# Modulation products in groups of four over the column quarters of TensorE, with a third weight buffer in the gating stage

## The chip, the cores and the metric

The kernel runs on one core of one Trainium2 chip, in one launch. The metric is the device time of that launch in microseconds (us). The time before is the median of three runs, 3602.42 us (3598.81 to 3608.07).

The engines are TensorE (PE; its weight loads are PEld), VectorE (DVE), ScalarE (ACT), GpSimd (POOL) and SyncE (SP). SP and POOL issue the DMAs that this text is about.

## What is computed

Two blocks of layers over 512 tokens of width 1024, all in float32. The first block is an attention layer (`mla`), a feed-forward layer, a spatial gating layer (`sgu`) and a second feed-forward layer. The second block has four layers (convolution, a linear recurrence, attention, convolution) over the 512 tokens and 256 context tokens. Each of these four takes a shift, a scale and a gate from a conditioning vector, and that modulation is what the change touches:

```python
def second_block(x, c, ctx, c_ctx, norm_g, mod_w, mod_b, ...):
    for i in range(DEPTH_2):                       # 4 layers
        shift, scale, gate = modulation(c, mod_w[i], mod_b[i])
        h = modulate(rmsnorm(x, norm_g[i]), shift[:, None], scale[:, None])
        if ctx_in:
            shift_c, scale_c, gate_c = modulation(c_ctx, mod_w[i], mod_b[i])
        ...
        x = x + gate[:, None] * y
```

`modulation` multiplies silu(c), 1024 numbers, with a matrix 1024 x 3072 and adds a bias; `c_ctx` goes the same way. For the four layers that is 4 x 12.6 MB of weights for very little arithmetic.

## The kernel before

Features lie on the 128 partitions, in 8 tiles (KT = 8). Most products are made in three float32r parts: the helper `wblk` (lines 87 to 97) loads a block of weights 128 x 1024 (0.5 MB) by SP, splits it on ACT (L93) and DVE (L94), and `mm3` (L121 to L123) multiplies high with high, high with low and low with high. One block is 24 matmuls of 128 x 512 (in `mla` some are fewer, in `sgu` one loop is written out, L754).

The modulation is a side stream. It does not depend on the tokens, so `set_filler` (lines 278 to 287) makes it a generator that each `wblk` of the main chain advances: by two steps in `mla` (layer 0 of the second block), by one step in `sgu` and the second feed-forward layer (layers 1 to 3, one after the other). Its weights are issued by POOL (L84, the helper `load`) into the pool `wst` of the side stream: three buffers in `mla`, two in `sgu`.

```python
    def modulation(self, s, l, pool, ps):                       # L302
        for k in range(KT):
            for b in range(3):
                w = s.load(A["mod_w"][l, k, :, b * 1024:(b + 1) * 1024])
                for h in range(2):
                    n = 2 * b + h
                    q = n % 4
                    nc.tensor.matmul(pm[n // 4][32 * q:32 * q + 32, :], self.cs[:, k, :], w[:, h * 512:(h + 1) * 512],
                                     start=k == 0, stop=k == KT - 1, skip_group_check=True)     # L312
                yield 1
```

A load holds 1024 of the 3072 columns for 128 input features. Each half of it is one product (L312): the stationary operand is `cs`, 128 x 32 (two of its 32 columns are the two vectors, the rest zero), the moving one 128 x 512 of the weights. The 32 output rows go to one of four groups of 32 partitions, q = 0 to 3, and with that the product uses one quarter of the array's columns. The six products of one k are q = 0 and 1, q = 2 and 3 in the PSUM tile `pm[0]`, and q = 0 and 1 in `pm[1]`. A float32 product stands in the trace as two matmul records, so two products are "x4" there. There are 4 layers x 24 loads x 2 = 192 products, 96 pairs.

At the end of a layer, ACT copies `pm` to SBUF (L318), four transposes for each of the two tiles follow (L321), and DVE adds the bias (L323).

The program is not in the order in which the code emits it: a scheduler inside the framework places each instruction on its engine's queue by its own estimates. Each engine then works through its queue in that fixed order, so a product that is not ready holds up what stands behind it on PE.

Other lines that the text names: L171 (`colsum`) and L180 (`rows`) are the two TensorE ends of a norm, with a chain of small DVE steps between them (L205, L156 to L162); L436 is a memset by POOL for the convolution that follows.

Of the kernel before, what the change touches and what calls it, by code (L numbers as in the profile page):

```python
# [7 lines left out]
F32 = mybir.dt.float32  # L8
F32R = mybir.dt.float32r
I32 = mybir.dt.int32  # L10
AF = mybir.ActivationFunctionType
# [6 lines left out]
KT = 8  # L18
# [33 lines left out]
class Stream:  # L52
    """Pools and helpers for a chain of layers over N tokens, features on the partitions."""
# [8 lines left out]
    def pools(self, nm, wst=0, whl=0, hp=0, tp=0, mm=0, W=None, hw=None):  # L62
        """Opens the pools that are asked for by their buffers."""
# [23 lines left out]
    def wblk(self, src, cols=1024, st=None):  # L87
        """A block of weights in float32, split exactly into two float32r parts."""
# [14 lines left out]
    def split(self, pr, src, scale=None, bias=None):  # L103
        """hi + lo = src * scale, or src + bias"""
# [20 lines left out]
    def lin(self, outs, w, acts, wo=0, ws=P, start=True, stop=True):  # L125
        """outs: [(PSUM part, columns of the tokens)]"""
        n = len(acts)
        for k, a in enumerate(acts):
            ww = tuple(x[:, wo + k * ws:wo + k * ws + P] for x in w)
            for o, c in outs:  # L130
                self.mm3(o, ww, (a[0][:, c], a[1][:, c]), start and k == 0, stop and k == n - 1)
# [9 lines left out]
    def group(self, ws, acts):  # L141
        """Several outputs at once, as the operands become ready."""
# [6 lines left out]
    def rsqrt(self, v, pool=None):  # L149
        """v ** -0.5 on a small tile [128, n]"""  # L150
# [14 lines left out]
    def colsum(self, tiles, N):  # L165
        """Sums over the features for each token: PSUM [128 tokens, N / 128]."""
# [8 lines left out]
    def rows(self, y, N, tag="rs", dst=None):  # L175
        """Columns y [128 tokens, N / 128] -> a row over all partitions [128, N]; in PSUM without a tag."""
# [33 lines left out]
class Kern:  # L210
# [17 lines left out]
    def open_x(self, n):  # L228
        """The two streams and the running sums of their squares."""
# [12 lines left out]
    def track(self, k, vi=0, acc=None, gain=1.0):  # L242
        """x[:, k] is final: its squares go into the sum for the next norm."""
# [14 lines left out]
    def both_rstd(self, s):  # L258
        """The norms of x and of the context in one chain."""
# [18 lines left out]
    def set_filler(self, gen, per=1):  # L278
        """Another chain of work, emitted in step with the blocks of weights of the main one."""
# [14 lines left out]
    # ------------------------------------------------------------- modulation  # L294
# [7 lines left out]
    def modulation(self, s, l, pool, ps):  # L302
        """shift, scale and gate of layer l, for both vectors, with the features on the partitions"""
        nc, A = self.nc, self.A
        pm = [ps.tile([P, 512], F32, name=f"pmod{i}", bufs=1) for i in range(2)]
        for k in range(KT):
            for b in range(3):
                w = s.load(A["mod_w"][l, k, :, b * 1024:(b + 1) * 1024])
                for h in range(2):
                    n = 2 * b + h  # L310
                    q = n % 4
                    nc.tensor.matmul(pm[n // 4][32 * q:32 * q + 32, :], self.cs[:, k, :], w[:, h * 512:(h + 1) * 512],  # L312
                                     start=k == 0, stop=k == KT - 1, skip_group_check=True)
                yield 1
        for g in range(2):
            nq = 4 if g == 0 else 2
            r = pool.tile([P, 512], F32, name="modr")
            nc.scalar.activation(out=r[:32 * nq], in_=pm[g][:32 * nq], func=AF.Copy)  # L318
            pt = ps.tile([P, 4, P], F32, name=f"pmod{g}", bufs=1)
            for j in range(4):  # L320
                nc.tensor.transpose(pt[:, j, :32 * nq], r[:32 * nq, j * P:(j + 1) * P], self.ident[:32 * nq, :32 * nq])  # L321
            for vi in range(2):
                nc.vector.tensor_tensor(  # L323
                    out=self.modv[:, l, vi, 16 * g:16 * g + 4 * nq].rearrange("p (q j) -> p q j", j=4),
                    in0=pt[:, :, :32 * nq].rearrange("p j (q r) -> p q j r", r=32)[:, :, :, vi],
                    in1=self.v("mod_b", 24 * l + 16 * g, 4 * nq).rearrange("p (q j) -> p q j", j=4), op=ALU.add)
# [5 lines left out]
    def mod_h(self, s, x, l, vi, rs=None, gs=None):  # L332
        """The modulated norm of x, split."""
# [17 lines left out]
    # -------------------------------------------------------------- conv layer  # L351
    def conv(self, s, x, l, j, vi):
# [3 lines left out]
        with self.tc.tile_pool(name=f"cv{N}", bufs=1, side=s.side, reuse_waits="tile") as cp, \  # L356
# [5 lines left out]
            for k in range(KT):  # L362
# [10 lines left out]
                # twice a * sigmoid(b)  # L373
# [18 lines left out]
            # layer norm over the features  # L392
# [25 lines left out]
            # the norm that the next layer starts from takes the place of the sums  # L418
# [3 lines left out]
    def conv_x(self, l, j):  # L422
        """The layer on x. The convolution runs in PSUM: some taps as diagonal matrices on TensorE, most on VectorE; the last ones are for ScalarE and GpSimd."""
        nc, A, s, x, N, H = self.nc, self.A, self.m, self.x, T, 15
        NPE, NPO, NG = 4, 7, 4
        with self.tc.tile_pool(name="cv", bufs=1, reuse_waits="tile") as cp, self.tc.tile_pool(name="cw", bufs=5, reuse_waits="tile") as cw, \
# [7 lines left out]
            def glu(k):  # L434
# [7 lines left out]
                # twice a * sigmoid(b)  # L442
# [60 lines left out]
            # layer norm over the features  # L503
# [23 lines left out]
    # ---------------------------------------------------------------- block 1  # L527
    def scaled(self, gname, gi):
        """x * gain, split"""
# [15 lines left out]
    def mla(self):  # L545
        nc, tc, A, s = self.nc, self.tc, self.A, self.m
        scale = 192.0 ** -0.5
        with tc.tile_pool(name="mla", bufs=1, reuse_waits="tile") as mp, tc.tile_pool(name="mla2", bufs=2, reuse_waits="tile") as m2, \
# [10 lines left out]
            # the first products wait in PSUM for the norm  # L559
# [6 lines left out]
            # rope tables: cos and signed sin of fl(position * inv_freq)  # L566
# [160 lines left out]
    def sgu(self):  # L727
        nc, tc, A, s = self.nc, self.tc, self.A, self.m
        with tc.tile_pool(name="sgu", bufs=1, reuse_waits="tile") as sp, tc.tile_pool(name="sgu2", bufs=2, reuse_waits="tile") as s2, \
                tc.tile_pool(name="sgu8", bufs=9, reuse_waits="tile") as s8, s.pools("m", hp=8, tp=2, mm=2), tc.tile_pool(name="pa", bufs=1, space=PSUM, reuse_waits="tile") as pa:  # L730
            # spatial weights, masked, and the sums of their rows
# [76 lines left out]
    def final_norm(self, s):  # L808
        """The norm at the end of the first block, and in one step with it the norm of the layer that follows."""
# [6 lines left out]
        # r1 = (m1 + eps) ** -0.5 and r1 * (r1 ** 2 * m2 + eps) ** -0.5 = (m2 + eps * (m1 + eps)) ** -0.5  # L816
# [16 lines left out]
    # -------------------------------------------------------------- rwkv layer  # L833
    # tokens of both sequences side by side: 256 of the context, then 512 of x; two halves of 384 in two banks
# [1067 lines left out]
```

## Time and profile before

| | |
|---|---|
| median of three runs | 3602.42 us |
| lowest, highest | 3598.81, 3608.07 us |
| span of the profiled execution | 3582.6 us |
| what lies around the span, against the median | 19.8 us |
| PE busy | 3409.4 us, 95% |
| DVE, ACT, POOL busy | 64%, 40%, 17% |

The profiled execution has no time of its own beside its span; the 19.8 us is the difference to the median. The page gives each engine's busy time, the span in 40 slices, the DMA queues, and groups of instructions by line. Matmuls are pipelined: one of 512 columns shows some 0.39 us, while the next starts 0.23 us after it, so distances between starts are what a matmul costs, not its length. "idle before <-" names what ended the wait of the engine.

Where the stages lie, in us from the span's start: `mla` to about 250, with its modulation products from 8 to 112; the first feed-forward layer to about 690; `sgu` to 1045; the second feed-forward layer to 1424, with modulation products to 1211.

### The profile page before, as it was taken

The page shows a single profiled execution, that of the slowest core. Times are in us where ns is not written, and L with a number is a line of the kernel's source. Part 1 is how long each engine was busy: PE and PEld are TensorE (multiplying, and loading weights), DVE is VectorE, ACT ScalarE, POOL GpSimd, SP SyncE. Part 2 cuts the span into 40 slices and gives each one's busy share as a digit, 9 for nine tenths or more (in the row PEclk, how much of TensorE's full clock was granted, in tenths as well). Part 3 has the DMA queues.
Part 4 walks back from the last instruction along what each step waited for, and adds up shares of the span by engine and source line. Part 5 has one row for each costly group of instructions (what it writes and reads, how often), then busy time and mean ns, then how long its engine had stood idle before and what let it go on. Part 6 is the DMA issues. An engine that isn't in the chain of part 4 may idle for free. (4 is left out here: it accounts for less than half of the span.)

```text
span 3582.6 us, 52130 instructions
## 1 busy us (share of the span) xinstructions
PE 3409.4 (95%) x20784; PEld 2778.1 (78%) x20784; DVE 2307.9 (64%) x3811; ACT 1448.9 (40%) x2336; POOL 603.8 (17%) x674
## 2 busy tenths in 40 slices
PE   7999999999999999998999979999889999999897
PEld 4678888767766787676988858888788788888676
DVE  4568875426443345887478788888452476666786
ACT  3443334323232233555356524333423254444553
POOL 1000000000000000763002231121110200000682
PEclk9999999999999999998999879999899999999999
DMA  6123333343444322221227772221421522211221
GB/s 246 44 89 107 111 117 113 136 142 136 152 143 157 120 98 94 71 77 65 95 101 227 240 208 82 84 87 49 175 92 42 182 71 80 71 62 46 91 73 57
DMA packets 201380, 396.94 MB, mean 111 GB/s; under 512 B 16624, under 2 KB 109552, under 8 KB 200112
## 3 DMA queue, kind: packets, MB, share of 16 engines
q1 hardware_dynamic: 161328, 287.56, 24.0%
q0 software_dynamic: 24880, 93.08, 7.8%
q10 hardware_dynamic: 14928, 12.98, 1.2%
q8 instruction: 163, 2.67, 0.3%
q14 instruction: 81, 0.66, 0.1%
HBM read 328.79 MB, written 58.46 MB: 108 GB/s over the span
## 5 line engine op out<-in xcount | busy, mean ns | idle before, releaser
L93 ACT ACTIVATE wh<-wst 128x1024 fp32r<-128x1024 f32 (+1 forms) x413 | 423.0, 1026 | 1100.5 <-PE pmm L122 728.8
L121 PE MATMUL pmm<-hh,wh 128*128 128x512 f32 (+1 forms) x1752 | 670.5, 384 | 4.2 <-ACT hh L108 3.6
L123 PE MATMUL pmm<-hh,wl 128*128 128x512 f32 (+1 forms) x1752 | 662.3, 379 | 4.3 <-POOL wl L94 4.3
L122 PE MATMUL pmm<-hl,wh 128*128 128x512 f32 (+1 forms) x1752 | 661.5, 378 | 2.7 <-DVE hl L109 1.9
L94 DVE TENSOR_TENSOR wl<-wst,wh 128x1024 fp32r<-128x1024 f32 (+1 forms) x347 | 406.8, 1173 | 348.8 <-ACT wh L93 348.3
L121 PEld LDWEIGHTS pmm<-hh,wh 128*128 128x128 f32 x1752 | 332.0, 190 | 90.5 <-ACT wh L93 13.4
L123 PEld LDWEIGHTS pmm<-hh,wl 128*128 128x128 f32 x1752 | 331.1, 189 | 73.1 <-POOL wl L94 6.0
L122 PEld LDWEIGHTS pmm<-hl,wh 128*128 128x128 f32 x1752 | 331.3, 189 | 67.5 <-issue 5.3
L465 DVE SCALAR_TENSOR_TENSOR acc<-yp,vec,acc 128x512 f32<-128x512 f32 x320 | 224.5, 751 | 20.6 <-PE acc L461 14.1
L94 POOL TENSOR_TENSOR wl<-wst,wh 128x1024 fp32r<-128x1024 f32 x66 | 161.5, 2460 | 425.7 <-ACT wh L93 405.3
L539 DVE TENSOR_TENSOR x<-pmm,x 128x512 f32<-128x512 f32 x88 | 60.7, 690 | 247.7 <-PE pmm L123 247.7
L121 PE MATMUL pmm<-uh,wh 128*128 128x512 f32 x512 | 200.5, 392 | 0.0
L123 PE MATMUL pmm<-uh,wl 128*128 128x512 f32 x512 | 199.7, 390 | 0.0
L122 PE MATMUL pmm<-ul,wh 128*128 128x512 f32 x512 | 199.3, 389 | 0.0
L84 POOL DMA_DIRECT2D wst<-mod_w x96 | 50.8, 530 | 562.7 <-PE pmod L312 512.4
L312 PE MATMUL pmod<-wst,cs 128*32 128x512 f32 x384 | 110.5, 657 | 19.1 <-DMA wst<-mod_w 18.9
L474 POOL TENSOR_TENSOR part<-part,tap 128x512 f32<-128x512 f32 x96 | 124.0, 1292 | 13.8 <-ACT part L472 7.5
L708 DVE SCALAR_TENSOR_TENSOR ft<-pmm,rs 128x512 f32<-128x512 f32 x64 | 44.0, 688 | 118.4 <-PE pmm L123 117.0
L381 DVE SCALAR_TENSOR_TENSOR Y<-yp,vec,Y 128x256 f32<-128x256 f32 x240 | 115.7, 482 | 6.2
L121 PEld LDWEIGHTS pmm<-uh,wh 128*128 128x128 f32 x512 | 96.2, 188 | 26.4 <-ACT wh L93 7.5
L123 PEld LDWEIGHTS pmm<-uh,wl 128*128 128x128 f32 x512 | 96.1, 188 | 20.2
L1177 PE MATMUL G<-KR,BK 128*128 128x256 f32 x384 | 102.0, 410 | 10.1 <-DMA KR<-krd 6.6
(673 smaller groups left out, 7503.5 us busy)
## 6 DMA issues: line engine op xcount, KB each, us to landing
wst<-mod_w POOLq DMA_DIRECT2D x96, 512.0 KB, 4.0
wst<-w_up SPq DMA_DIRECT2D x64, 512.0 KB, 3.2
wst<-w_down SPq DMA_DIRECT2D x64, 512.0 KB, 3.2
wst<-conv_in SPq DMA_DIRECT2D x48, 512.0 KB, 3.2
wst<-conv_in POOLq DMA_DIRECT2D x24, 512.0 KB, 3.6
BK<-bkd SPq DMA_DIRECT2D x48, 256.0 KB, 2.9
KR<-krd SPq DMA_DIRECT2D x96, 128.0 KB, 3.3
krd<-kr SPq DMA_DIRECT2D x14, 768.0 KB, 4.3
```

What stands on the lines that cost most here:

```text
L84: self.dma.dma_start(out=st, in_=src)
L93: nc.scalar.activation(out=hi, in_=st, func=AF.Copy)
L94: (nc.gpsimd if self.pool_lo else nc.vector).tensor_tensor(out=lo, in0=st, in1=hi.bitcast(F32), op=ALU.subtract)
L121: nc.tensor.matmul(out, w[0], a[0], start=start, stop=False)
L122: nc.tensor.matmul(out, w[0], a[1], start=False, stop=False)
L123: nc.tensor.matmul(out, w[1], a[0], start=False, stop=stop)
L312: nc.tensor.matmul(pm[n // 4][32 * q:32 * q + 32, :], self.cs[:, k, :], w[:, h * 512:(h + 1) * 512], start=k == 0, stop=k == KT - 1, skip_ ...
L381: nc.vector.scalar_tensor_tensor(out=acc, in0=yp[:, i:i + N], scalar=wc, in1=acc, op0=ALU.mult, op1=ALU.add)
L465: nc.vector.scalar_tensor_tensor(out=accs[k], in0=yps[k][:, i:i + N], scalar=weight(k, i), in1=accs[k], op0=ALU.mult, op1=ALU.add)
L474: nc.gpsimd.tensor_tensor(out=part, in0=part, in1=t, op=ALU.add)
L539: self.nc.vector.tensor_tensor(out=self.x[:, m], in0=pt, in1=self.x[:, m], op=ALU.add)
L1177: nc.tensor.matmul(G[:, 2 * q:2 * q + 2].rearrange("p e x -> p (e x)"), BK[:, d, i, m].rearrange("p a t -> p (a t)"), KR[:, d, i, m].rearr ...
```

## The change

The products are regrouped into quads. A quad is two loads, that is four products, placed on q = 0, 1, 2, 3: the two loads of columns 0 to 2047 of one k, and for the last 1024 columns the loads of two neighbouring k together. Those last columns so accumulate in two sums, even k on q = 0 and 1, odd k on q = 2 and 3, which are added at the end (one more DVE instruction for each vector). The four products of a quad are emitted one after the other, one load behind: after the first load of the next quad. The generator has one step more for each layer (26 instead of 25). The copy takes all 128 partitions of both tiles into a buffer of the pool `wst`, in place of a pool of its own. In `sgu` the pool `wst` has three buffers instead of two. The program's comments are gone, so line numbers move: L312 is L316 after the change, L321 is L336, L323 is L340 and L342.

```diff
-    def modulation(self, s, l, pool, ps):
+    def modulation(self, s, l, ps):
         pm = [ps.tile([P, 512], F32, name=f"pmod{i}", bufs=1) for i in range(2)]
-        for k in range(KT):
-            for b in range(3):
-                w = s.load(A["mod_w"][l, k, :, b * 1024:(b + 1) * 1024])
+        quads = []
+        for k in range(0, KT, 2):
+            quads += [[(k, 0), (k, 1)], [(k + 1, 0), (k + 1, 1)], [(k, 2), (k + 1, 2)]]
+
+        def products(quad, ws):
+            for n, ((k, b), w) in enumerate(zip(quad, ws)):
                 for h in range(2):
-                    n = 2 * b + h
-                    q = n % 4
-                    nc.tensor.matmul(pm[n // 4][32 * q:32 * q + 32, :], self.cs[:, k, :], w[:, h * 512:(h + 1) * 512],
-                                     start=k == 0, stop=k == KT - 1, skip_group_check=True)
+                    q = 2 * n + h
+                    nc.tensor.matmul(pm[b // 2][32 * q:32 * q + 32, :], self.cs[:, k, :], w[:, h * 512:(h + 1) * 512],
+                                     start=k < (1 if b < 2 else 2), stop=k >= KT - (1 if b < 2 else 2), skip_group_check=True)
+
+        wait = None
+        for quad in quads:
+            ws = []
+            for k, b in quad:
+                if ws and wait:
+                    products(*wait)
+                ws.append(s.load(A["mod_w"][l, k, :, b * 1024:(b + 1) * 1024]))
                 yield 1
+            wait = quad, ws
+        products(*wait)
+        yield 1
         for g in range(2):
             nq = 4 if g == 0 else 2
-            r = pool.tile([P, 512], F32, name="modr")
-            nc.scalar.activation(out=r[:32 * nq], in_=pm[g][:32 * nq], func=AF.Copy)
+            r = s.wst.tile([P, 1024], F32, name="wst")[:, :512]
+            nc.scalar.activation(out=r, in_=pm[g], func=AF.Copy)
             pt = ps.tile([P, 4, P], F32, name=f"pmod{g}", bufs=1)
             for j in range(4):
-                nc.tensor.transpose(pt[:, j, :32 * nq], r[:32 * nq, j * P:(j + 1) * P], self.ident[:32 * nq, :32 * nq])
+                nc.tensor.transpose(pt[:, j], r[:, j * P:(j + 1) * P], self.ident)
...
+                if g == 1:
+                    nc.vector.tensor_tensor(out=mv, in0=part(2), in1=mv, op=ALU.add)
...
-                with f.pools("f", wst=2), tc.tile_pool(name="fm", bufs=1, side="right", reuse_waits="tile") as fm, \
-                    tc.tile_pool(name="fmp", bufs=1, space=PSUM, side="right", reuse_waits="tile") as fmp:
-                    K.set_filler((x for l in range(1, 4) for x in K.modulation(f, l, fm, fmp)))
+                with f.pools("f", wst=3), tc.tile_pool(name="fmp", bufs=1, space=PSUM, side="right", reuse_waits="tile") as fmp:
+                    K.set_filler((x for l in range(1, 4) for x in K.modulation(f, l, fmp)))
                     K.sgu()
```

How the scheduler places the products is seen on PE's queue. First, the second feed-forward layer, between two blocks of weights of the main chain (`uh`, `ul` are its operands, `pmod` the sums of the modulation). Before, such a place stands after every 24 matmuls:

```order
L123 MATMUL pmm<-uh,wl 128x512
L312 MATMUL pmod_8215<-wst,cs 32x512 x2
L121 MATMUL pmm<-uh,wh 128x512
L122 MATMUL pmm<-ul,wh 128x512
L123 MATMUL pmm<-uh,wl 128x512
```

Of the change, where it stands after every 48:

```order
L123 MATMUL pmm<-uh,wl 128x512
L316 MATMUL pmod_8290<-wst,cs 32x512 x4
L121 MATMUL pmm<-uh,wh 128x512
L122 MATMUL pmm<-ul,wh 128x512
L123 MATMUL pmm<-uh,wl 128x512
```

Two insertions of two products have become one of four.

Second, the first norm of `mla`, between its two TensorE ends L171 and L180. Before (`pmod_140` is `pm[0]`, `pmod_141` is `pm[1]`):

```order
L171 MATMUL pmm<-cst,sx_75 128x1 x4
L312 MATMUL pmod_140<-wst,cs 32x512 x2
L312 MATMUL pmod_141<-wst,cs 32x512 x2
L312 MATMUL pmod_140<-wst,cs 32x512 x4
L312 MATMUL pmod_141<-wst,cs 32x512 x2
L180 MATMUL pmm<-cst,rs_y 128x128 x4
L121 MATMUL pmm<-hh,wh 128x512
L122 MATMUL pmm<-hl,wh 128x512
L312 MATMUL pmod_140<-wst,cs 32x512
```

Of the change (`pmod_137` is `pm[0]`, `pmod_138` is `pm[1]`):

```order
L171 MATMUL pmm<-cst,sx_75 128x1 x4
L316 MATMUL pmod_138<-wst,cs 32x512 x3
L316 MATMUL pmod_137<-wst,cs 32x512 x6
L180 MATMUL pmm<-cst,rs_y 128x128 x4
L121 MATMUL pmm<-hh,wh 128x512
L122 MATMUL pmm<-hl,wh 128x512
L316 MATMUL pmod_137<-wst,cs 32x512 x2
```

Between the two ends stand nine products instead of ten. The last of them needs the ninth load in both programs.

Third, the last quad of layer 2 of the second block, at the end of `sgu` and the start of the next layer, a quad that the scheduler split. Before, in that place:

```order
L312 MATMUL pmod_7070<-wst,cs 32x512 x2
L321 MATMUL pmod_8159<-cst,modr 128x128 x4
L121 MATMUL pmm<-hh,wh 128x512
L122 MATMUL pmm<-hl,wh 128x512
L123 MATMUL pmm<-hh,wl 128x512
```

Of the change:

```order
L123 MATMUL pmm<-gh,wl 128x512
L316 MATMUL pmod_7098<-wst,cs 32x512 x4
L316 MATMUL pmod_7099<-wst,cs 32x512
L121 MATMUL pmm<-hh,wh 128x512
L316 MATMUL pmod_7099<-wst,cs 32x512
L122 MATMUL pmm<-hl,wh 128x512
```

One quad stands whole, with the first product of the next behind it; the second product follows one matmul later, and the other two 20 matmuls after that.

## Rows read from the trace of the kernel before

**Rows 1.** The page: TensorE in 40 equal slices, busy tenths and granted clock.
```profile
PE   7999999999999999998999979999889999999897
PEclk9999999999999999998999879999899999999999
```

**Rows 2.** Stretches: engines' busy us (instructions), PEclk, DMA share, GB/s.
```profile
0.00:112.00 112.00, 92.66 (x351) 50.42 (x352) 49.83 (x113) 45.02 (x73) 13.30 (x29) 0.92 0.60 213
690.00:1213.00 523.00, 517.55 (x2239) 361.30 (x2238) 217.86 (x353) 145.88 (x191) 42.48 (x90) 0.99 0.42 147
1213.00:1330.00 117.00, 117.00 (x521) 96.64 (x520) 45.89 (x56) 32.04 (x38) 0.00 (x0) 1.00 0.28 96
```

**Rows 3.** Line 312 on the page; PE's waits, 690 to 1213: us, times, longest.
```profile
L312 PE MATMUL pmod<-wst,cs 128*32 128x512 f32 x384 | 110.5, 657 | 19.1 <-DMA wst<-mod_w 18.9
...
PE pmm L180 <- DVE rs_y L162: 3.9, 2, 2.5
...
PE pmod L312 <- DMA wst<-mod_w: 0.7, 1, 0.7
```

**Rows 4.** Order of time on PE: start us, length us; one pair in the gating stage.
```profile
885.30 0.39 PE L122 MATMUL pmm<-gl,wh 128*128 128x512 f32 x1
885.53 0.40 PE L123 MATMUL pmm<-gh,wl 128*128 128x512 f32 x1
885.86 1.05 PE L312 MATMUL pmod<-wst,cs 128*32 128x512 f32 x4
886.84 0.51 PE L121 MATMUL pmm<-gh,wh 128*128 128x512 f32 x1
887.18 0.39 PE L122 MATMUL pmm<-gl,wh 128*128 128x512 f32 x1
```

**Rows 5.** The same view: one, three, four and six products together.
```profile
85.61 1.04 PE L312 MATMUL pmod<-wst,cs 128*32 128x512 f32 x2
...
825.65 1.06 PE L312 MATMUL pmod<-wst,cs 128*32 128x512 f32 x6
...
1050.49 1.07 PE L312 MATMUL pmod<-wst,cs 128*32 128x512 f32 x8
...
57.60 1.92 PE L312 MATMUL pmod<-wst,cs 128*32 128x512 f32 x12
```

**Rows 6.** The same view: the norm at the start of the gating stage.
```profile
723.35 0.95 PE L171 MATMUL pmm<-cst,sx 128*128 128x1 f32 x8
724.22 1.06 PE L312 MATMUL pmod<-wst,cs 128*32 128x512 f32 x8
727.83 1.09 PE L180 MATMUL pmm<-cst,rs_y 128*128 128x128 f32 x4 [2.54 <-DVE rs_y L162]
729.66 3.18 PE L312 MATMUL pmod<-wst,cs 128*32 128x512 f32 x8 [0.74 <-DMA wst<-mod_w]
```

**Rows 7.** Order of time, attention layer; last, a stretch: PE busy, PEclk, DMA share, GB/s.
```profile
28.66 1.92 PE L312 MATMUL pmod<-wst,cs 128*32 128x512 f32 x12
33.81 3.20 PE L312 MATMUL pmod<-wst,cs 128*32 128x512 f32 x8 [3.23 <-DMA wst<-mod_w]
36.94 1.12 PE L180 MATMUL pmm<-cst,rs_y 128*128 128x128 f32 x4
...
73.33 1.92 PE L312 MATMUL pmod<-wst,cs 128*32 128x512 f32 x4 [0.15 <-DMA wst<-mod_w]
76.76 1.04 PE L312 MATMUL pmod<-wst,cs 128*32 128x512 f32 x2 [1.51 <-DMA wst<-mod_w]
...
73.30:75.30 2.00, 1.92 (x4) 0.50 0.89 320
```

**Rows 8.** The page, DMA issues: KB each, median us from issue to landing.
```profile
wst<-mod_w POOLq DMA_DIRECT2D x96, 512.0 KB, 4.0
```

**Rows 9.** Lines 321 and 323: ns min/median/max, first and last start us, shapes.
```profile
L321 PE MATMUL pmod<-cst,modr x32: 221/272/329, 111.9 to 1218.0; 128*128 128x128 f32 x16, 64*128 64x64 f32 x16
...
L323 DVE TENSOR_TENSOR modv<-pmod,vec x16: 153/162/175, 199.9 to 1218.4; 128x16 f32<-128x16 f32 x8, 128x8 f32<-128x8 f32 x8
```

More of the change, by code (lines that the diff above doesn't have):

```diff
@@ L320, in modulation @@
             for j in range(4):
-                nc.tensor.transpose(pt[:, j, :32 * nq], r[:32 * nq, j * P:(j + 1) * P], self.ident[:32 * nq, :32 * nq])
+                nc.tensor.transpose(pt[:, j], r[:, j * P:(j + 1) * P], self.ident)
             for vi in range(2):
[L323 to L326, printed above, removed]
+                mv = self.modv[:, l, vi, 16 * g:16 * g + 4 * nq].rearrange("p (q j) -> p q j", j=4)
@@ L327, in modulation @@
+                part = lambda q: pt[:, :, 32 * q:32 * (q + nq)].rearrange("p j (q r) -> p q j r", r=32)[:, :, :, vi]
+                nc.vector.tensor_tensor(out=mv, in0=part(0), in1=self.v("mod_b", 24 * l + 16 * g, 4 * nq).rearrange("p (q j) -> p q j", j=4), op=ALU.add)
+                if g == 1:
+                    nc.vector.tensor_tensor(out=mv, in0=part(2), in1=mv, op=ALU.add)
         for vi in range(2):
@@ L1742, in build @@
             K.mod_start(csp)
-            with f.pools("f", wst=3), tc.tile_pool(name="fm", bufs=1, side="right", reuse_waits="tile") as fm, \
-                    tc.tile_pool(name="fmp", bufs=1, space=PSUM, side="right", reuse_waits="tile") as fmp:
-                K.set_filler(K.modulation(f, 0, fm, fmp), 2)
+            with f.pools("f", wst=3), tc.tile_pool(name="fmp", bufs=1, space=PSUM, side="right", reuse_waits="tile") as fmp:
+                K.set_filler(K.modulation(f, 0, fmp), 2)
                 K.mla()
@@ L1754, in build @@
             if run("sgu"):
-                with f.pools("f", wst=2), tc.tile_pool(name="fm", bufs=1, side="right", reuse_waits="tile") as fm, \
-                    tc.tile_pool(name="fmp", bufs=1, space=PSUM, side="right", reuse_waits="tile") as fmp:
-                    K.set_filler((x for l in range(1, 4) for x in K.modulation(f, l, fm, fmp)))
+                with f.pools("f", wst=3), tc.tile_pool(name="fmp", bufs=1, space=PSUM, side="right", reuse_waits="tile") as fmp:
+                    K.set_filler((x for l in range(1, 4) for x in K.modulation(f, l, fmp)))
                     K.sgu()
```

## The prediction, as it was put on record before the changed kernel ran

> **What bounds the kernel now.** I read the slices first: PE is busy for nine tenths or more nearly everywhere in the first 16 of 40 slices, where the modulation runs, at the granted clock's full level (2.4 GHz) but for dips in the attention layer [rows 1]. The table of stretches says the same by stage. In the gating stage and the second feed-forward layer (690 to 1213 us) PE is busy 517.6 of 523 us, DVE 218, ACT 146, and the DMA engines 0.42 of the time; right after the last modulation product (1213 to 1330) the same layer goes on with PE at 117 of 117 us [rows 2]. PE's waits in the first of these are 3.9 us for the DVE steps of two norms, 0.7 for a modulation load [rows 3], and little else. So from 690 to 1213 us PE alone sets the time, and what leaves PE's queue there leaves the sum. In `mla` (0 to 112 us) PE is busy only 92.7 us, the DMA engines 0.60 and the clock 0.92 [rows 2]: there the products also wait for loads and for norms, and the order on PE decides.
>
> **What a group of products costs.** In the order of time, ordinary matmuls start 0.23 us apart. Around a pair the starts are 885.53, 885.86, 886.84 and 887.18 [rows 4]: 1.65 us where two ordinary steps would be 0.46, so the pair displaces 1.19 us. In the feed-forward layer the same reading gives 1.18; I use 1.18. The rows on group size decide the case: one product alone is as long as a pair (1.04 us), three are 1.06, four on the four quarters 1.07 [rows 5]. The scheduler already made three such fours by chance, where one pair's q = 2, 3 met the next one's q = 0, 1, or two loads met. Only when a quarter comes round again does a second round begin: six products take 1.92, that is 0.87 more [rows 5]. A quad therefore costs 1.18 + 0.02 us against 2.36 for its two pairs.
>
> The rule of the Trainium skill to weigh against this is in TensorE: Matmul & The Clock Gate, section "Measured speedup vs the span model". It lists 2.38 times for three column tiles and 3.07 times for four row tiles, not three and four times. By 3.07, which no row here shows, a quad would last 1.30 of one product; the estimate is 1.04 x 0.30 = 0.3 us more for each of 36 quads, 11 us less gain. The rows of one, three and four products stand against it with a growth of 3%.
>
> **Sum for 690 to 1213 us.** I count places on PE's queue where products interrupt the main chain, leaving out those inside a norm (between L171 and the work after L180).
> - Before: layer 1 has 21 places, layer 2 has 24, layer 3 has 22, together 67. Most are pairs; a few are singles that cost the same.
> - After: 12, 12 and 12, together 36. Most hold a whole quad; layer 1 has four quads cut in two (1 + 3), partly joined to a neighbour, and the last quad of layer 2 is cut in three.
> - 67 - 36 = 31 places fewer, by 1.18: 36.6 us off.
> - One place of the change holds five products (the third pair of fences above), so a second round: 0.9 us on. The wider quads: 36 x 0.02 = 0.7 us on.
> - The norm at 723 us: before, PE is held from 724.2 to 732.8, the last 3.18 us by a second four, long as products at half the clock [rows 6]. After, six products stand ahead of L180 and two behind; those two need a load that can be issued only when the quad at 724 has freed a buffer. Issue 0.5 and landing 4.0 [rows 8] put it at 729, and one round at a granted clock of 0.50 (1.2 GHz), 1.92 [rows 7], ends near 731: 1.5 us off. Ends: 0 to 3.
> - Copy, transposes and additions: the second tile's transposes grow from 64 to 128 columns, 0.22 to 0.27 us [rows 9], 12 of them; DVE gets six more steps of 0.16 us here. Taken as 0.5 us on. The DVE part is covered by PE, except near a norm.
>
> Together 36 us off.
>
> **POOL, SP and the third buffer.** In a quad only the second load has to wait for the quad before. With 48 matmuls of 0.23 us between quads, 11 us, against 0.5 + 4.0 for issue and landing [rows 8], it is there in time, and the other load has still longer. That is why the third buffer is costed at nothing: it pays for holding two loads at once, and if it were late by more than 6 us the cover would be gone. On POOL the memsets of L436 now come two loads earlier in the queue. They wait for the end of the gating stage's last readers; the load behind them, in turn, needs the quad that comes after that point on PE, so the wait ends in time. SP's queue keeps its order. After the second feed-forward layer the order on every engine is as before, so later stages move as a whole.
>
> **Sum for `mla`.** This is the less certain term.
> - First norm: before, L180 starts at 36.94, after two waits in a row that the ninth load ends [rows 7]. After, PE is free of the first products about 2 us sooner (four products instead of six stand ahead of the first block), but the ninth load is again the last thing before L180. I take 2 us off.
> - Behind it two lone products become one place: 1.2 us off.
> - After the third norm: before, products hold PE from 73.33 to 77.8, with a wait of 1.51 for a load [rows 7]. After, one round of four stands there, whose loads are issued earlier: about 2.4 us off. Ends: 0 to 3.4.
> - The rest: 9 places instead of 10: 1.2 us off.
>
> These come to 6.8 us. Since DVE, ACT and the loads share the end of this stage, I take 5. The bounds are 3 us slower (each quad now waits for two loads, and one wait for a load here is 3.23 [rows 7]) and 9 us faster.
>
> **The number.** 36 + 5 = 41 us off the profiled execution, 3582.6 to 3541.6 for the span; with the 19.8 us around it, and so against the median, 3602.4 - 41 = **3561 us**.
>
> **Rivals.**
> 1. *The quarters share less than the short rows say.* If four products on end made two rounds, each of the 36 quads would cost 1.18 + 0.87 against 2.36, 0.3 saved. Scaled from the sum, 31 x 1.18 becomes about 36.6 - 36 x 0.87 = 5 us, and with `mla` at 3 the time is 3594. Against it: the fours at 724 and 1050 [rows 5, 6]. For it: only three cases, none followed directly by a 128-column matmul. Chance 0.03. By the rule cited above the time is 3572; this milder form lies inside the range and has 0.05.
> 2. *Slower: the quad waits for its second load.* That load can be issued only when the quad before has freed its buffer. If the time from one quad to the next fell under the 4.5 us of issue and landing, or landing stretched past 11 us, PE would stand at every quad. The point from which this decides is 1.2 us of waiting for each quad, where the gain is gone; at 2 us each, 36 x 0.8 = 29 us, the time is 3631. For it: in `mla`, with little work between the groups, just such waits of 3.2 us and the fallen clock after them stand in the rows [rows 7]. Against it: 11 us of matmuls between quads from 690 us on, and only 0.7 us of such waiting there before [rows 3]. Chance 0.02.
> 3. *Hidden gain.* If another engine were close behind PE, taking 36 us from PE would only uncover it. DVE at 218 and ACT at 146 of 523 us [rows 2] are far off. Together with losses in `mla` that eat the gain, the time would be about 3597. Chance 0.03.
> 4. *The scheduler's quads are not all whole when run.* A quad whose halves are cut in two costs a place more; these are counted already, since the order is fixed. What is open is only whether neighbours in `mla` cost what they did: 3552 to 3573. This is my forecast's own spread.
>
> **Chances.** Forecast as above 0.87, the milder form of rival 1 0.05, rivals 1 to 3 0.08. A measurement of this kernel can tell about 0.3% (11 us) from no change. Faster by more than that, under 3591.6: 0.92 (forecast and milder form). Within it: rivals 1 and 3, 0.06. Slower: rival 2, 0.02. The range: the sum's own bounds are 36 with 30 to 40 (the price of a place known to 0.02, the norm and the small terms by 3 each way) and `mla` with -3 to 9, so 27 to 49 us off at the extremes, 3553 to 3575; the runs before lie from 3.6 under to 5.7 over their median, which adds some 5 us each way. I give 3548 to 3580.
>
> **What would show it.** In the profile after: L316 in one group of 192 products with PE busy on it down from 110.5 us [rows 3] to about 60; quads "x8" of 1.07 us with the next matmul starting 1.00 after them; places every 11 us from 750 us on; no wait of PE for `mod_w` after 735 us; the last product near 1180 instead of 1210 us; the stretches behind unchanged in length. The step is wrong if quads are longer than 1.2 us, if PE waits for DMA at quads, or if the last modulation product comes early while the layer's end does not.

## The result, and the profile after

The changed kernel takes 3552.2 us (median of 4 runs, 3542.5 to 3555.98), the kernel before 3605.24 us beside it (4 runs, 3598.81 to 3620.07): ratio 0.986, 95% interval 0.9833 to 0.9886. A second measurement gives 0.9865 (0.9843 to 0.9887). The forecast was 3561 us, with a range of 3548 to 3580.

The span of the profiled execution and its mean granted clock, of before and then of after:

```profile
core 0: 3582.6 us, clock 0.965
```
```profile
core 0: 3554.2 us, clock 0.963
```

The profiled execution of after has a time of 3555.98 us, so only 1.8 us lie around a span. The profiled execution of before was thus one of some 3584 us: what I called "around the span" was the distance of a fast execution to the median.

The group of products of after, from the view by line and from the page's form of it, which answers to [rows 3]; then PE's waits in the gating stage and the second feed-forward layer:

```profile
L316 PE MATMUL pmod<-wst,cs x384: 592/617/1062, 9.3 to 1186.3; 128*32 128x512 f32 x192
...
  DMA wst<-mod_w: 34.4, 18
```
```profile
L316 PE MATMUL pmod<-wst,cs 128*32 128x512 f32 x384 | 75.2, 635 | 17.0 <-DMA wst<-mod_w 16.9
```
```profile
PE pmm L180 <- DVE rs_y L162: 2.8, 2, 1.6
PE pmod L316 <- DMA wst<-mod_w: 1.2, 1, 1.2
PE pmm L121 <- DVE rs_y L162: 0.4, 1, 0.4
```

PE is busy with products for 75.2 us instead of 110.5, and the last one starts at 1186.3 instead of 1210.0. PE waits for a modulation load once from 690 us on, at 724.

The same two stretches as in [rows 2], then the products' own share of the first, of after and (behind it) of before:

```profile
690.00:1213.00 523.00, 518.52 (x2410) 390.50 (x2410) 231.03 (x376) 154.20 (x198) 41.37 (x88) 1.00 0.44 153
1213.00:1330.00 117.00, 117.00 (x518) 96.89 (x517) 48.56 (x55) 36.85 (x46) 0.00 (x0) 1.00 0.29 99
...
690.00:1213.00 523.00, 43.14 (x288) 6.49 (x288) 1.00 0.44 153
```
```profile
690.00:1213.00 523.00, 75.78 (x288) 10.33 (x288) 0.99 0.42 147
```

PE is as full as before. In the same 523 us it now issues 2410 matmuls instead of 2239, 288 of them products in both: the 32.6 us that the products gave up hold main-chain work. PE bounds this stretch before and after.

One quad in the gating stage, order of time on PE (as in [rows 4]):

```profile
886.26 0.40 PE L123 MATMUL pmm<-gh,wl 128*128 128x512 f32 x1
886.59 1.07 PE L316 MATMUL pmod<-wst,cs 128*32 128x512 f32 x8
887.58 0.51 PE L121 MATMUL pmm<-gh,wh 128*128 128x512 f32 x1
887.93 0.39 PE L122 MATMUL pmm<-gl,wh 128*128 128x512 f32 x1
```

From 886.26 to 887.93 are 1.67 us, 1.65 around the pair in [rows 4]: four products displace what two did.

How far the two traces are apart is read at matmuls of the main chain that both programs have: the start in after less that in before, at the time of before.

| before, us | 125 | 689 | 722 | 735 | 1044 | 1213 | 1330 | 2000 | 2700 | end |
|---|---|---|---|---|---|---|---|---|---|---|
| after, us | -3.6 | -2.0 | -5.5 | -8.4 | -28.8 | -42.4 | -40.1 | -33.2 | -28.9 | -28.5 |

The last residual addition of the second feed-forward layer, of before and of after (the last number before the semicolon is its start):

```profile
L539 DVE TENSOR_TENSOR x<-pmm,x x88: 681/691/693, 206.3 to 1424.1; 128x512 f32<-128x512 f32 x88
```
```profile
L555 DVE TENSOR_TENSOR x<-pmm,x x88: 681/691/693, 201.1 to 1384.0; 128x512 f32<-128x512 f32 x88
```

So 40 us are gained up to 1330 us, where the products run, and 41 were forecast. (The last two quads of the change stand behind the matmul of 1213 us, which is why the gain falls from 42.4 to 40.1.) Behind, in code that is unchanged and in the same order, the trace of after is 11.6 us longer. One place of this is the stretch 2150 to 2300 us (columns as in [rows 2]), here of before, of after, and of two kernels of the experiments with the same code there, `before_again` and `quads_mla_only`:

```profile
2150.00:2300.00 150.00, 143.63 (x2188) 128.88 (x2188) 130.67 (x226) 58.74 (x155) 28.61 (x39) 0.99 0.27 84
```
```profile
2150.00:2300.00 150.00, 143.99 (x2124) 128.22 (x2122) 126.35 (x219) 54.65 (x140) 24.88 (x34) 0.94 0.27 82
```
```profile
2150.00:2300.00 150.00, 144.41 (x2164) 128.99 (x2162) 129.19 (x223) 57.41 (x150) 27.36 (x37) 0.97 0.27 84
```
```profile
2150.00:2300.00 150.00, 144.58 (x2009) 128.28 (x2006) 124.98 (x223) 54.19 (x143) 24.99 (x33) 0.92 0.25 79
```

PE is as busy in all four, but the granted clock is 0.99, 0.94, 0.97 and 0.92, and the lowest has the fewest matmuls. These windows are equal in time; between the same two matmuls, those of 2150 and 2300 us in the first, the other three take 6.5, 1.5 and 9.6 us longer. How much of this stretch runs at the lower level differs from execution to execution.

### The profile page after: what moved, and what is told of

Read it like the earlier page. It is cut to its first block, busy times and chain, and to the rows that moved or that the text cites. A ratio compares the mean times of both kernels' runs of the same rounds, so it can differ in the third digit from the quotient of the medians.

```text
span 3554.2 us, 52157 instructions
## 1 busy us (share of the span) xinstructions
PE 3380.8 (95%) x20784; PEld 2784.5 (78%) x20784; DVE 2308.4 (65%) x3819; ACT 1448.9 (41%) x2336; POOL 604.6 (17%) x674
## 5 line engine op out<-in xcount | busy, mean ns | idle before, releaser
L122 PEld LDWEIGHTS pmm<-ul,wh 128*128 128x128 f32 x512 | 96.1, 188 | 19.0
```

Source lines behind the costliest of these rows:

```text
L122: nc.tensor.matmul(out, w[0], a[1], start=False, stop=False)
```

## The experiments

In the table, deltas are against the first trace of before as above (the first trace of before ends its feed-forward layer at 1424.1); "FFN end" is the start of the last residual addition. Where one run is given, it is the profiled one, and there is no ratio.

| kernel | median us (runs) | ratio, 95% interval | FFN end | 125 | 735 | 1330 | end |
|---|---|---|---|---|---|---|---|
| after_again | 3556.11 (5) | 0.9865, 0.9843 to 0.9887 | 1386.9 | -3.8 | -5.6 | -37.2 | -23.0 |
| pairs_wst3 | 3602.53 (12) | 0.9998, 0.9978 to 1.0019 | 1422.2 | -1.1 | -3.0 | -1.9 | +5.0 |
| four_on_two | 3591.41 (12) | 0.997, 0.9955 to 0.9985 | 1425.7 | +2.5 | +4.7 | +1.6 | +11.6 |
| quads_wst2 | 3559.32 (6) | 0.9877, 0.9852 to 0.9902 | 1385.2 | -3.9 | -5.8 | -38.9 | -16.6 |
| quads_gating_only | 3564.99 (4) | 0.9896, 0.9864 to 0.9928 | 1393.2 | +2.3 | +0.1 | -30.8 | -18.8 |
| quads_wst2_per2 | 3574.25 (8) | 0.992, 0.9894 to 0.9945 | 1403.4 | -1.4 | +0.5 | -20.6 | -2.4 |
| quads_per4 | 3598.8 (1) | | 1417.0 | -5.3 | +5.7 | -7.1 | +14.4 |
| pairs_last_k | 3539.45 (1) | | 1375.3 | +5.0 | +15.5 | -48.8 | -45.0 |
| quads_mla_only | 3595.06 (12) | 0.999, 0.9974 to 1.0006 | 1420.1 | -6.3 | -3.9 | -4.0 | +5.4 |
| before_again | 3583.95 (1) | | 1421.8 | -3.0 | -2.3 | -2.3 | -0.5 |
| before_again2 | 3585.95 (1) | | 1423.5 | -1.1 | -0.6 | -0.6 | +1.5 |

**The changed kernel again** (no edit).

> The changed kernel once more, to part the gain from the scatter of single executions. Theory A (fewer places on TensorE's queue, and four quarters in one round): the last residual addition of the second feed-forward layer starts near 1384 us again (1424 before), and the ratio over several runs is 0.988, that is 40 to 45 us off. Theory C (part of the measured 0.986 is luck of the clock): the part up to 1384 us repeats within 2 us, while the stages behind it differ by up to 10 us from profile to profile, with the granted clock.

It repeats the gain; its trace stands 36.6 us further ahead at 1330 than at 689, the first one 38.1.

**The third buffer alone**, with pairs.

```diff
-            r = pool.tile([P, 512], F32, name="modr")
+            r = s.wst.tile([P, 1024], F32, name="wst")[:, :512]
...
-                with f.pools("f", wst=2), ...
+                with f.pools("f", wst=3), ...
```

> The kernel before with a third weight buffer in the gating stage and the feed-forward layer behind it, products still in pairs, and the copy of the sums in a weight buffer, as in the change. Theory A: no gain, the second feed-forward layer ends at 1424 us within 3, ratio to before 0.997 to 1.003; PE still has 67 to 69 places outside norms there. Theory B (the third buffer, which lets loads start earlier, gives a part of the gain): the layer ends 5 us or more before 1424, ratio under 0.998.

Worth nothing: ratio 0.9998, and no gain between 735 and 1330.

**Groups of four, but on two quarters.** As many places as the change has, with two rounds in each.

```diff
-            quads += [[(k, 0), (k, 1)], [(k + 1, 0), (k + 1, 1)], [(k, 2), (k + 1, 2)]]
+            quads += [[(k, b), (k + 1, b)] for b in range(3)]
...
-                    q = 2 * n + h
+                    c = 2 * b + h
+                    q = c % 4
```

> The changed kernel with groups of four products on two quarters: the two loads of a group are the same columns of two neighbouring k, so products 1 and 3, and 2 and 4, fall on the same quarter and go in two rounds. Places on PE's queue are as few as in the change (36 outside norms). Theory A: each place costs one round of 0.87 us more than in the change, some 33 places, so the second feed-forward layer ends at 1384 + 29 = 1413 us, and a group shows 1.92 us instead of 1.07; ratio to before 0.995 to 0.998. Theory D (only the number of interruptions counts, not the quarters): it ends at 1384 to 1387 us, ratio 0.988.

One group of it, order of time on PE:

```profile
1101.83 0.39 PE L123 MATMUL pmm<-hh,wl 128*128 128x512 f32 x1
1102.15 1.91 PE L317 MATMUL pmod<-wst,cs 128*32 128x512 f32 x8
1103.99 0.50 PE L121 MATMUL pmm<-uh,wh 128*128 128x512 f32 x1
```

From the matmul before to the one behind it takes 2.16 us, 1.32 around the quad above: the second round costs 0.84 (0.87 was taken for it). Here the second round also adds to the same sums as the first; but the six products of [rows 5] go to six different sums and take 1.92 as well, so it is the quarter used twice that costs. From 735 to 1330, with 35 places in both, this kernel gains 3.1 us, the changed one 31.7. Fewer places alone give a tenth of the gain; sharing the round gives the rest. The layer ends some 12 us later than the 1413 that was expected. About 6 of that are the attention layer (+2.5 at 125 us, against -3.6), and about as much the norm at the start of the gating stage:

```profile
730.59 1.05 PE L317 MATMUL pmod<-wst,cs 128*32 128x512 f32 x4 [1.05 <-DMA wst<-mod_w]
735.63 1.92 PE L317 MATMUL pmod<-wst,cs 128*32 128x512 f32 x2 [4.00 <-DMA wst<-mod_w]
737.48 0.80 PE L769 MATMUL pv<-wh,hh 128*128 128x512 f32 x1
```

Products that need two late loads hold PE from 730.59 to 737.48, the second time for 4.00 us of waiting.

**Two buffers**, the products right behind the second load.

```diff
-        wait = None
...
-                if ws and wait:
-                    products(*wait)
                 ws.append(s.load(A["mod_w"][l, k, :, b * 1024:(b + 1) * 1024]))
+                if len(ws) == 2:
+                    products(quad, ws)
                 yield 1
-            wait = quad, ws
-        products(*wait)
-        yield 1
...
-                with f.pools("f", wst=3), ...
+                with f.pools("f", wst=2), ...
```

> The change with two weight buffers in the gating stage and the next layer, the products of a quad put right behind its second load, in the attention layer too. Theory A: both loads of a quad then wait for the quad before, but have 11 us on PE against 0.5 + 0.5 + 4 us for issue and landing, so the third buffer is worth nothing there: the second feed-forward layer ends at 1383 us within 3, no wait of PE for mod_w between 735 and 1185 us, ratio 0.988. Theory B (the third buffer is needed to have two loads ready): PE waits at most quads, and the layer ends later than 1390 us.

The gain from 689 to 1330 is the same, 36.6 us, and from 690 to 1213 PE waits once for a load, 0.9 us. At this distance between quads, 12 us from one start to the next in a dense stretch, neither the third buffer nor the lag is needed.

**Quads in layers 1 to 3 only**; `mla` keeps the code of before (its generator as a second function).

```diff
-                K.set_filler(K.modulation(f, 0, fmp), 2)
+                K.set_filler(K.modulation0(f, 0, fm, fmp), 2)
                 K.mla()
```

> The change for layers 1 to 3 alone (gating stage and the feed-forward layer behind it); layer 0, in the attention layer, in pairs as before. Theory A: at 330 us it stands where the kernel before stands, within 1 us, and the second feed-forward layer ends 36 us before 1424, at 1388 within 2; so the attention layer's part of the gain is 3 to 4 us. Theory C: whatever is gained or lost after 1450 us goes with the granted clock, not with the change.

From 689 to 1330 it gains 34.7 us, against 36 forecast for this part and 38.1 and 36.6 in the two traces of the change. It ends later than expected (1393.2, not 1388), mostly by what it stood behind at 689, +3.9; at 330 us it stands 2.3 behind, where 1 was expected at most.

**Quads closer together: two steps for each block**, with the edit of quads_wst2 (two buffers, no lag). This is rival 2's mechanism, but with both loads of a quad waiting for the quad before.

```diff
-                    K.set_filler((x for l in range(1, 4) for x in K.modulation(f, l, fmp)))
+                    K.set_filler((x for l in range(1, 4) for x in K.modulation(f, l, fmp)), 2)
```

> Two weight buffers, and two steps of the modulation for each block of weights in the gating stage, so quads stand every 24 matmuls, 6.7 us apart, and both loads of a quad are issued only behind the quad before. Theory A: issue of two loads and landing, 1.0 + 4.0 us, are still under 6.7, so PE does not wait in the steady part, places outside norms are 34 to 38, and the second feed-forward layer ends at 1384 to 1389 us. Theory B (the lead that a third buffer gives is what makes quads free): PE waits for mod_w at most quads, 20 us or more in all, and the layer ends after 1400.

Quads now stand 6.8 us apart, from one start to the next where they are closest. Three of them, order of time on PE:

```profile
760.63 1.07 PE L316 MATMUL pmod<-wst,cs 128*32 128x512 f32 x8
761.62 0.50 PE L766 MATMUL pv<-wh,hh 128*128 128x512 f32 x1
...
774.25 1.85 PE L316 MATMUL pmod<-wst,cs 128*32 128x512 f32 x8
776.03 0.50 PE L766 MATMUL pv<-wh,hh 128*128 128x512 f32 x1
...
910.93 1.05 PE L316 MATMUL pmod<-wst,cs 128*32 128x512 f32 x4
912.55 1.05 PE L316 MATMUL pmod<-wst,cs 128*32 128x512 f32 x4 [0.56 <-DMA wst<-mod_w]
913.53 0.50 PE L121 MATMUL pmm<-gh,wh 128*128 128x512 f32 x1
```

The first is whole. In the other two the second half starts late, because its load does. Little of this shows as waiting of PE (4.3 us); what the quads from 746 us on take over 0.99 adds up to some 7.5 us, and the weight loads ahead of all products from 690 us on (PEld, which overlaps PE) wait 10.8 us:

```profile
PEld pmod L316 <- DMA wst<-mod_w: 10.8, 14, 2.3
```

Against quads_wst2 it loses 6.6 us from 689 to 746, where it has 11 places instead of 5 (6 x 1.13 = 6.8), and another 9.1 from 746 to 1330, although it has 30 places there instead of 33. The layer ends at 1403.4, beyond the 1384 to 1389 that Theory A gave. So a load that comes late does cost, as rival 2 had it; with 12 us from quad to quad it isn't late.

**Still closer: four steps, three buffers.**

```diff
-                    K.set_filler((x for l in range(1, 4) for x in K.modulation(f, l, fmp)))
+                    K.set_filler((x for l in range(1, 4) for x in K.modulation(f, l, fmp)), 4)
```

> The change with four steps of the modulation for each block of weights in the gating stage: two quads for each block, some 3.3 us apart, less than the 4.5 us from the issue of a quad's second load to its landing. Most quads stand cut in two on PE's queue (50 places outside norms instead of 36). Theory A: 14 places more cost 17 us and PE waits for mod_w 10 to 40 us in all: the second feed-forward layer ends between 1405 and 1440 us. Theory D (only the quads' concurrency counts, not when the loads land): it ends under 1395.

Quads are cut in two, and the halves stand apart:

```profile
799.42 1.06 PE L316 MATMUL pmod<-wst,cs 128*32 128x512 f32 x8
...
801.97 1.05 PE L316 MATMUL pmod<-wst,cs 128*32 128x512 f32 x4
...
804.78 1.05 PE L316 MATMUL pmod<-wst,cs 128*32 128x512 f32 x4
```

At 1330 us it stands 33 us behind the change. 52 places instead of 39 (inside norms included) are 15 of them by the price of 1.18. The products' waits for loads, 48.6 us in the whole trace against 34.4 above, are at most another 14: this figure adds the waits of PE to those of the weight loads, which overlap. The rest is open.

**Pairs, with 7 of 8 products of layers 1 to 3 left out** (only k = 7 is multiplied; all weights are loaded).

```diff
+                    if l and k < KT - 1:
+                        continue
...
-                                     start=k == 0, stop=k == KT - 1, skip_group_check=True)
+                                     start=k == 0 or l > 0, stop=k == KT - 1, skip_group_check=True)
```

> The kernel before with the products of layers 1 to 3 left out but for those of the last eighth of the features; all loads are kept. It leaves out seven eighths of the modulation's arithmetic in these layers, so that the price of the places is measured alone. Theory A: of 67 places outside norms some 6 are left, so 61 x 1.18 = 72 us less, and the norm at 723 us costs 3 to 5 us less: the second feed-forward layer ends at 1347 to 1352 us. Theory E (a part of the places fills waits of PE, for loads or for the vector engines): less than 60 us come off, and PE shows new waits in these stages.

Its feed-forward layer ends 23 to 28 us later than expected. It stands 15.5 us behind at 735, by the attention layer (+5.0 at 125) and one new wait at the start of the gating stage, of PE for the masking of the spatial weights (`wsp`) by POOL:

```profile
PE pmm L743 <- POOL wsp L739: 11.2, 1, 11.2
```

The rest is that 57 places fell away and not 61, each for less: from 735 to 1330 there are 6 instead of 63, and it gains 64.3 us, 1.13 each. (The change, 35 instead of 63, gains 31.7 in the same stretch: 1.13 each.)

**The kernel before, twice again**, and **quads in `mla` only** (`mla` as changed, layers 1 to 3 with the code and the two buffers of before).

> The kernel before, profiled a second time. Theory A (the 12 us that the changed kernel gives back after 1330 us are the difference between two executions of the same later stages, and the profiled execution of before was a fast one): against that first execution the same matmuls come within 3 us of each other between 735 and 1330 us, and from 1330 us to the end 5 to 20 us later; the span lies between 3587 and 3605 us. Theory B (the change makes the later stages slower): the later stages stand within 2 us of the first execution, span 3580 to 3585 us.

> The same a third time, for how far two executions of the same code differ in the attention layer. Theory A: from -1 to +5 us at the matmul of 125 us, as in four kernels with the attention layer of before, and 5 to 20 us from 1330 us to the end. Theory B: within 1 us at 125 us and within 2 us after 1330 us.

```diff
-                    K.set_filler((x for l in range(1, 4) for x in K.modulation(f, l, fmp)))
+                    K.set_filler((x for l in range(1, 4) for x in K.modulation0(f, l, fm, fmp)))
                     K.sgu()
```

> Quads in the attention layer alone; layers 1 to 3 with the pairs and the two buffers of before. Theory A (the attention layer is worth the 5 us of the prediction): 3594 us (3590 to 3597), ratio 0.9986; at the matmul of 125 us the trace stands 3 to 5 us ahead of the first execution of before, and nothing is gained from 735 to 1330 us. Theory B (it is worth nothing, the difference at 125 us is between executions): ratio 1.000, 3599 us, at 125 us between -1 and +5. Theory C (what the changed kernel has over the one with quads in the gating stage alone, 3556 against 3565 us, is all the attention layer's): 3590 us, ratio 0.9975.

My Theory A failed in the two repetitions: the profiled executions of before agree within 2 us at the end (spans 3582.2 and 3584.2, clock 0.965 both), so the first was no exception among the profiled ones, and by the letter the traces came out as Theory B had it. It doesn't hold for the times, though. Over the 53 executions of before that have a clock on record, profiled and not, the time runs from 3582.58 to 3616.94 us and goes with the mean granted clock (0.967 to 0.957; correlation -0.90). One slope for the 116 executions of eight kernels gives 3.05 us for each 0.001 of the clock; at the same clock the change is then 40.3 us faster than before, quads_wst2 37.1, quads_gating_only 37.8, quads_wst2_per2 27.1, four_on_two 5.3, quads_mla_only 3.2, and pairs_wst3 3.0 slower. Without a fit: at 0.965 two executions of the change took 3548.26 and 3549.25 us, six of before 3582.58 to 3593.55, on average 3587.8, 39 us more. The profiled execution of before had 0.965 where the 53 have 0.9615 on average, by the slope some 11 us; that of the change had 0.963, about the average of its own. This is most of the difference between 28.5 us in the traces and 43 to 53 in the medians. The executions of the change also had 0.002 more on average than those of before, some 6 us of the 43 to 53 that are not its own gain. At the same clock nothing is given back in the later stages: 40.3 us, against 40.1 in the trace at 1330.

quads_mla_only was too small a change for its timing (-4 us, interval on both sides of 1). At the same clock it is 3.2 us faster, and its trace stands 6.3 us ahead at 125 us.

## Why the prediction was right, and where it wasn't

**What bounds the kernel**: right. The stretch from 690 to 1213 is PE's before and after, and neither DVE nor ACT came up (231 and 154 of 523 us). One reading was off without harm: the slices of [rows 1] show no dip of the clock in the attention layer; it is the 0.92 of [rows 2] that does.

**Price of a place and of a quad**: right. 1.18 was taken for a place, less 2.1 us in all for the place of five, the wider quads and the copies: 34.5 us for 31 places fewer. Measured are 3.5 us from 689 to 722 (3 places fewer) and 31.7 from 735 to 1330 (28 fewer), together 35.2, or 1.14 each after all deductions. A quad shares its round, 1.07 us, and four_on_two shows what it would cost otherwise. That settles rival 1 and its milder form. By the Trainium skill (TensorE: Matmul & The Clock Gate, section "Measured speedup vs the span model") I had weighed 3.07 times, its figure for four row tiles. Here four products take 1.07 us where one takes 1.04 [rows 5], 3.9 times. The measurement decides: that figure doesn't carry over to these four column quarters.

**690 to 1213 us, 36 us forecast**: 38.1 and 36.6 from 689 to 1330 in the traces of the change, 34.7 in quads_gating_only. What differs between them is the norm at 723, forecast at 1.5 us with ends of 0 and 3. Here it is in the first trace of the change, and behind it the late round alone in after_again and in quads_gating_only:

```profile
722.24 0.65 PE L180 MATMUL pmm<-cst,rs_y 128*128 128x128 f32 x4 [1.61 <-DVE rs_y L162]
724.07 1.05 PE L316 MATMUL pmod<-wst,cs 128*32 128x512 f32 x4 [1.18 <-DMA wst<-mod_w]
725.05 0.50 PE L770 MATMUL pv<-wh,hh 128*128 128x512 f32 x1
```
```profile
725.52 1.92 PE L316 MATMUL pmod<-wst,cs 128*32 128x512 f32 x4 [1.26 <-DMA wst<-mod_w]
```
```profile
730.32 1.92 PE L316 MATMUL pmod<-wst,cs 128*32 128x512 f32 x4 [1.57 <-DMA wst<-mod_w]
```

From 722 to 735 they gain 2.9, 1.5 and 0.2 us, and the two repetitions of before 0.9 and 1.0 over its first trace. The late load comes earlier than the 729 that I had worked out, at 724. The round behind it takes 1.05 us in the first trace, but in the two others 1.92, as forecast (after_again has a granted clock of 0.76 from 722 to 728 us, the first trace 1.00). On average the three gain 0.9 us against the three traces of before, within the ends of 0 and 3; the first pair alone, with 2.9, makes the term look too small.

**The attention layer, 5 us forecast**: of the right size, as far as it can be told, by the average of several traces. At 125 us the four traces with the changed `mla` (after, after_again, quads_per4, quads_mla_only) stand at -3.6 to -6.3, -4.8 on average; six with pairs there (the three of before, pairs_wst3, quads_gating_only, pairs_last_k) at -3.0 to +5.0, +0.4 on average. On the same averages 2.5 us are gained around the third norm, where 2.4 were forecast. Of the 5.2 us 4.0 are left at 689, and the times at the same clock give 2.5 (the change against quads_gating_only) and 3.2 (quads_mla_only against before). One pair of traces could not have shown it. The sub-term of the first norm, 2 us, looks wrong between the two first traces, since L180 starts at 37.72 instead of 36.94 [rows 7]:

```profile
28.86 2.16 PE L316 MATMUL pmod<-wst,cs 128*32 128x512 f32 x6
31.20 1.05 PE L316 MATMUL pmod<-wst,cs 128*32 128x512 f32 x4 [0.17 <-DMA wst<-mod_w]
34.27 1.05 PE L316 MATMUL pmod<-wst,cs 128*32 128x512 f32 x4 [2.02 <-DMA wst<-mod_w]
36.26 1.53 PE L316 MATMUL pmod<-wst,cs 128*32 128x512 f32 x4 [0.94 <-DMA wst<-mod_w]
37.72 1.12 PE L180 MATMUL pmm<-cst,rs_y 128*128 128x128 f32 x4
```

But 36.94 was the earliest of the six with pairs (36.9 to 40.0, 39.0 on average), and the four others start at 36.1 to 37.8, 37.1 on average: 1.9 us. The waits for loads are there, as feared in rival 2, and no longer than before.

**The third buffer at nothing**: right, twice (pairs_wst3, quads_wst2), at this distance between quads. The memsets of L436 (L452 after the change) show no cost either: POOL waits 4.5 us there, 5.0 before.

**"In time" for the second load**: right with 11 us of matmuls between quads. The cover is thinner than the 6 us that I gave: with quads 6.8 us apart, where two issues and a landing (0.5 + 0.5 + 4.0) leave 2 us, halves already start up to 1.6 us late. The page's median landing of these loads is 4.7 us there, and 4.8 in the changed kernel, instead of 4.0 [rows 8].

**"Later stages move as a whole"**: the order does, the time doesn't. This step failed for the trace: I forecast a span of 3541.6, and 3554.2 were measured. In the times it didn't matter, as shown above: at the same clock the whole gain is there.

**19.8 us around the span**: a wrong reading, see above. It did no harm to the forecast only because I took the gain off the median.

**Signs**: L316 was to fall to about 60 us and fell to 75.2. In 690 to 1213 it fell as it should, by 32.6; in the attention layer the products fell only from 34.7 to 32.0, as they lie apart there waiting for loads. The quads came every 12 us, not 11, as their own length comes on top, and the stretches behind were not unchanged in the trace. The other signs came as put: quads of 1.07 us with the next matmul 0.99 behind, one wait for `mod_w` and none after 735, the last product at 1186.

## What to carry to other kernels

Where one engine is full, price a small side stream by its interruptions and read from the trace which members of a group share a round: here 31 interruptions fewer at 1.14 us were 35 of the 40 us gained, and the grouping without the sharing was worth a tenth of it. Keep the groups far enough apart for the last load of each; closer together, the halves come apart and the wait hides in the length of the group, not in a line on waits. Before the time of one trace is set against a median, look at the mean granted clock of both; and before a term of 2 us is read from two traces, repeat one of them.

## What was not expected of the hardware

Time and granted clock of this program go together closely: 0.957 to 0.967 in 53 executions of one kernel, over 34 us of time. How much falls to the lower level (1.2 GHz) differs in one stretch, as the 0.92 to 0.99 of 2150 to 2300 us show. The executions come from three sets, whose means lie between 3598.7 and 3600.4 us, so the spread is inside each set. Profiled executions of before lay at the fast end three times in three. What decides it wasn't tried and stays open.

Entering and leaving the products costs the same for one, two or four, among matmuls of 512 columns: 0.32 or 0.33 us to the first product where two ordinary starts lie 0.23 apart, 0.34 or 0.35 after the first matmul behind it. The Trainium skill (TensorEngine Tiling (Array Packing), section "Key Properties") says that changing the tiling mode drains TensorE. The rows agree in that both sides of the group are 0.1 us longer; no run here separates the drain from the rest.
